# Rate at which VectorE's modulation steps are given out: 1.05 per projection tile instead of 0.7

## The chip, the cores and the metric

One core of a Trainium2 chip runs the whole kernel. The metric is the device time of one execution in microseconds (us), the median of several. Engines: TensorE (PE, with its weight loads as PEld), VectorE (DVE), ScalarE (ACT), GpSimd (POOL), and SyncE (SP), whose queue issues nearly all loads from HBM.

## The reference

Two layers, three groups of 128 tokens (one prompt group, two groups of latents, 384 tokens in all), width 1024, all in float32. What matters here:

```python
# mod = silu(c) @ ada_w[l] + ada_b[l], for two conditioning vectors: c_ctx (prompt), c (latents)
shift1, scale1, gate1, shift2, scale2, gate2 = jnp.split(mod[:, None, :], 6, axis=-1)
h = x * (1.0 + scale1) + shift1
mix, new_state = mixing_sublayer(h, p, init, latent)
x = layer_norm(DEEPNORM_ALPHA * x + gate1 * mix, p['ln1_w'], p['ln1_b'])
h = x * (1.0 + scale2) + shift2
a, gt = jnp.split(h @ p['ffn_w13'], 2, axis=-1)
ff = (jax.nn.silu(gt) * a) @ p['ffn_w2']
x = layer_norm(DEEPNORM_ALPHA * x + gate2 * ff, p['ln2_w'], p['ln2_b'])
```

`mod` of layer 1 depends on nothing but the conditioning vectors and the weights, so it can be computed at any time before layer 1 starts. It is a product of two vectors with a 1024 x 6144 matrix.

## The kernel before

**Products in two halves.** Every weight tile is split into a high and a low part in float32r: ScalarE casts the raw tile (`whi`, line 220), VectorE subtracts (`wlo`, line 221). TensorE then makes three matmuls where one would do (lines 270 to 272: high x high, low x high, high x low). A tile `wlo` is either 8 x 128 columns, made by two instructions of 128 x 512 from two raw tiles (`wcols`), or 2 x 512 columns, made by one instruction of 128 x 1024 (`wrows`). There are 3 buffers of raw tiles (`wraw`), 5 of `whi`, 4 of `wlo`.

**The FFN of a layer** runs in three parts of 8, 6 and 8 blocks of 128 hidden channels. Each part is `ffn_in` (columns of `ffn_w13` in chunks of 256: two tiles of the gate, then two tiles of the linear half, 24 matmuls of 384 columns each) and then `proj` (two halves of the output, three token groups each, 512 columns per matmul). For a gate tile ScalarE computes `sig`; for a linear tile VectorE multiplies (`gf`, line 1050), ScalarE casts (`fAh`) and VectorE subtracts (`fAl`, line 221). In `proj` VectorE multiplies the result by the gate vector (`gmix`, line 516) and adds it to `x` (lines 518 and 520).

**Layer 1's modulation on VectorE.** Two thirds of layer 1's `mod` (columns 0 to 4095, that is b = 0 and b = 1 of three) are not computed on TensorE but accumulated on VectorE while layer 0's FFN runs. The work is cut into 32 units. A unit loads 512 KB of `ada_w` (`wadv`, line 425, two buffers under the tag `wada`) and makes four instructions on VectorE: for each of 2 rows of 128 input channels and 2 conditioning vectors, accumulate weight x scalar into `adacc` (the first two of a group are line 477, all others line 479). Four units make one group of 512 columns. `close` then sums a group over partitions on TensorE (line 434, eight matmuls), the fourth group adds the bias (`mrows`, line 442), and `fin` transposes on TensorE (line 455) and copies to `modT` (line 456). The load of a unit is issued by the step of the unit before it:

```python
units = [(b, g, k) for b in bs for g in range(4) for k in range(0, KT, 2)]
...
                if k == 2 and i >= 4:
                    close(*units[i - 4][0:2])
            return go

        adq.extend(one(i) for i in range(len(units)))
        adq.extend([lambda: None, lambda: close(*units[-1][0:2]), lambda: None, lambda: None])
```

That is 36 steps in the queue `adq`, and two `fin` steps that are put into it on the way: 38. The third part (b = 2) is made on TensorE during layer 1 (`ada_steps`, lines 389 and 392).

**What sets the order.** The code emits instructions in program order; `tick` runs after every tile of a product and emits steps from `adq` by the rate `ADV`. The framework then places the instructions on the engines: an instruction whose operands are ready in its plan may be placed ahead of earlier ones, and the resulting order on each engine and on the SP queue is fixed. So the rate sets where a step is emitted, and the placement can move it some way from there.

```python
rate["aacc"] += w * rate["ada"]
while rate["aacc"] >= 1.0:
    rate["aacc"] -= 1.0
    if adq:
        adq.pop(0)()
```

The rate is set after the first `ffn_in` of layer 0. From there the ticks are 6 (first `proj`), 12 (second `ffn_in`), 6 (second `proj`), 16 (third `ffn_in`): 40. Before the last `proj` of layer 0 whatever is left in the queue is emitted at once:

```python
while adq:
    adq.pop(0)()
```

Of the kernel before, what the change touches and what calls it, by code (L numbers as in the profile page):

```python
# [33 lines left out]
M6 = 11  # L34
WRAW = 3
WADA = 2
ADV = 0.7
TAPS1, TAPS2 = 2.6, 3.2
FILL = 0.3
LEADN = 4  # L40
# [60 lines left out]
def tile_kernel(ctx: ExitStack, tc: tile.TileContext, a: dict, o: list):  # L101
# [1096 lines left out]
    for l in range(DEPTH):  # L1198
# [20 lines left out]
        for k0, n in ((0, 8), (8, 6), (14, 8)):  # L1219
            fA = ffn_in(l, h2, k0, n, lead if k0 == 0 else None)  # L1220
            if l == 0:
                rate["ada"] = ADV
            if lc2 is None:
# [58 lines left out]
```

## Time and profile before

| | |
|---|---|
| median of 3 runs | 1459.12 us (1458.92 to 1459.28) |
| the profiled execution, its own time | 1461.46 us |
| its span, first to last instruction | 1458.9 us |
| PE busy in the span | 1414.8 us |
| DVE busy in the span | 1004.5 us |
| mean granted TensorE clock | 0.989 of full speed |

The profile is of one execution. A duration of a matmul there overlaps the next one; the distance from start to start is what a matmul costs in a stream. The granted clock is 1.00 at 2.4 GHz and 0.50 at 1.2 GHz. Layer 0's FFN ends, and the last `proj` of layer 0 begins, some 720 us into the span.

### The profile page before, as it was taken

How to read it: one execution, taken by the hardware profiler on the slowest of the kernel's cores; microseconds unless marked ns; L12 is line 12 of the kernel's file. 1: busy time of each engine (PE TensorE's matmuls, PEld its weight loads, DVE VectorE, ACT ScalarE, POOL GpSimd, SP SyncE). 2: the span in 40 equal slices, each digit the busy share in tenths (PEclk: the TensorE clock that was granted, in tenths of full speed). 3: DMA queues.
4: the chain of work that ended last, by engine and by line, in shares of the span. 5: the costliest groups of instructions: out<-in, count | busy, mean ns of one | idle time of the engine just before them, and what ended most of it. 6: DMA issues, size and time to landing. Idle time of an engine off the chain costs nothing.

```text
span 1458.9 us, 20684 instructions
## 1 busy us (share of the span) xinstructions
PE 1414.8 (97%) x7990; PEld 1296.2 (89%) x7990; DVE 1004.5 (69%) x1976; ACT 590.2 (40%) x1090; POOL 67.5 (5%) x106
## 2 busy tenths in 40 slices
PE   6999999999999999999799999899999999999997
PEld 4799999989998999989677999899999889898996
DVE  3455798987987656897674559879886666544447
ACT  2445458423535333333134465544335254242430
POOL 1000002000100000000100010110000000000000
PEclk8999999999999999999899999999999999999999
DMA  9575254465473444666655442342535526243441
GB/s 323 170 233 177 95 138 158 144 230 175 160 273 101 150 162 136 217 189 202 217 143 165 154 149 66 84 123 87 164 99 170 173 73 205 86 157 100 145 159 43
DMA packets 141745, 226.09 MB, mean 155 GB/s; under 512 B 13304, under 2 KB 63032, under 8 KB 141648
## 3 DMA queue, kind: packets, MB, share of 16 engines
q1 hardware_dynamic: 140048, 222.65, 47.6%
q0 software_dynamic: 1600, 2.14, 0.5%
q8 instruction: 62, 1.02, 0.3%
q14 instruction: 35, 0.29, 0.1%
HBM read 221.05 MB, written 3.71 MB: 154 GB/s over the span
## 4 chain that ended last, share of the span: by engine, by line
PE 82%; DVE 9%; DMA 5%; ACT 1%; issue 1%; POOL 1%; SPq 0%; DVEq 0%; POOLq 0%; ACTq 0%
PE ps L270 24%; PE ps L271 24%; PE ps L272 24%; DMA wraw<-in_in_w_dram 3%; DVE wlo L221 2%; PE adaps L392 1%; DMA wadv<-in_ada_w_dram 1%; DVE cacc L870 1%; PE vacc L270 1%; PE vacc L271 1%; PE vacc L272 1%; DMA wada<-in_ada_w_dram 1%; DMA adaq<-in_ada_w_dram 1%; DVE adacc L479 1%; PE adaps L1108 1%
## 5 line engine op out<-in xcount | busy, mean ns | idle before, releaser
L220 ACT CAST whi<-wraw 128x512 fp32r<-128x512 f32 (+1 forms) x484 | 337.5, 723 | 591.9 <-PE ps L271 223.0
L221 DVE TENSOR_TENSOR wlo<-wraw,whi 128x512 fp32r<-128x512 f32 (+1 forms) x484 | 383.3, 813 | 176.2 <-ACT whi L220 75.6
L270 PE MATMUL ps<-h1h,whi 128*128 128x384 f32 x896 | 305.9, 342 | 4.6 <-DVE rpa L820 2.8
L272 PE MATMUL ps<-h1h,wlo 128*128 128x384 f32 x896 | 300.3, 336 | 1.0 <-DVE wlo L221 0.9
L271 PE MATMUL ps<-h1l,whi 128*128 128x384 f32 x896 | 299.6, 335 | 0.0
L270 PE MATMUL ps<-h2h,whi 128*128 128x384 f32 x576 | 193.4, 336 | 0.0
L272 PE MATMUL ps<-h2h,wlo 128*128 128x384 f32 x576 | 192.5, 334 | 0.0
L271 PE MATMUL ps<-h2l,whi 128*128 128x384 f32 x576 | 192.4, 334 | 0.0
L270 PEld LDWEIGHTS ps<-h1h,whi 128*128 128x128 f32 x896 | 168.4, 188 | 20.1 <-issue 8.4
L272 PEld LDWEIGHTS ps<-h1h,wlo 128*128 128x128 f32 x896 | 168.4, 188 | 2.1 <-DVE wlo L221 2.0
L271 PEld LDWEIGHTS ps<-h1l,whi 128*128 128x128 f32 x896 | 168.5, 188 | 0.1
L870 DVE SCALAR_TENSOR_TENSOR cacc<-u,cwt,cacc 128x399 f32<-128x399 f32 x232 | 144.7, 629 | 1.8
L270 PEld LDWEIGHTS ps<-h2h,whi 128*128 128x128 f32 x576 | 108.1, 188 | 1.1 <-issue 1.0
L271 PEld LDWEIGHTS ps<-h2l,whi 128*128 128x128 f32 x576 | 108.1, 188 | 0.2
L272 PEld LDWEIGHTS ps<-h2h,wlo 128*128 128x128 f32 x576 | 108.1, 188 | 0.0
L270 PE MATMUL ps<-whi,fAh 128*128 128x512 f32 x264 | 104.2, 395 | 0.0
L271 PE MATMUL ps<-wlo,fAh 128*128 128x512 f32 x264 | 103.8, 393 | 0.0
L272 PE MATMUL ps<-whi,fAl 128*128 128x512 f32 x264 | 103.7, 393 | 0.0
L516 DVE TENSOR_TENSOR gmix<-ps,lnc 128x512 f32<-128x512 f32 x48 | 33.1, 689 | 79.9 <-PE ps L272 79.9
L479 DVE SCALAR_TENSOR_TENSOR adacc<-wadv,cs,adacc 128x512 f32<-128x512 f32 x112 | 78.7, 746 | 4.4 <-DMA wadv<-in_ada_w_dram 4.4
L270 PEld LDWEIGHTS ps<-whi,fAh 128*128 128x128 f32 x264 | 50.3, 190 | 12.1 <-issue 1.9
L272 PEld LDWEIGHTS ps<-whi,fAl 128*128 128x128 f32 x264 | 50.1, 190 | 10.6
(318 smaller groups left out, 2019.4 us busy)
## 6 DMA issues: line engine op xcount, KB each, us to landing
wraw<-in_in_w_dram SPq DMA_DIRECT2D x64, 1024.0 KB
wraw<-in_ffn_w_dram SPq DMA_DIRECT2D x76, 512.0 KB
wraw<-in_ffn_w_dram SPq DMA_DIRECT2D x28, 1024.0 KB
wada<-in_ada_w_dram SPq DMA_DIRECT2D x48, 512.0 KB
wadv<-in_ada_w_dram SPq DMA_DIRECT2D x32, 512.0 KB
wraw<-in_out_w_dram SPq DMA_DIRECT2D x8, 1024.0 KB
adaq<-in_ada_w_dram SPq DMA_DIRECT2D x8, 512.0 KB
wraw<-in_mlstm_out_w_dram SPq DMA_DIRECT2D x4, 1024.0 KB
```

The lines of the kernel that those rows point to most:

```text
L220: nc.scalar.copy(hi, src)
L221: tt(lo, src, hi.bitcast(F32), op=ALU.subtract)
L270: mm(out, sh, vh, start=(first and i == 0), stop=False)
L271: mm(out, sh, vl, start=False, stop=False)
L272: mm(out, sl, vh, start=False, stop=(last and i == n - 1))
L392: mm(st["ps"][32 * g:32 * g + 32, :], cs[:, k, :], wts[g], start=(k == 0), stop=(k == KT - 1))
L479: stt(ac[:, m, :], wt[:, kk, :], c_, ac[:, m, :], op0=ALU.mult, op1=ALU.add)
L516: tt(g, ps, lc[0 if t == 0 else 1, hf], op=ALU.mult)
L870: tc.keep_in_program_order(stt(ac, u[:, k:k + CW], wk, ac, op0=ALU.mult, op1=ALU.add))
L1108: mm(ps[32 * g:32 * g + 32, s * 256:(s + 1) * 256], cs[:, k, :], tiles[u // 6][:, u % 6, :], start=(k < 4), stop=(k >= 4))
```

## The change

```diff
-ADV = 0.7
+ADV = 1.05
```

With 40 ticks, 0.7 gives out 28 of the 38 steps and 1.05 gives out all of them, the last at the 37th tick (37 x 1.05 = 38.85). No instruction is added or taken away: each engine has the same number before and after. Their order is the same up to the last tile of the first `proj` and again from the last `proj` on.

**Place 1, the end of the third `ffn_in` and the start of the last `proj`, on TensorE.** `ps_6655` is the last tile of `ffn_in`, `ps_6787` the first of `proj`. Before:

```order
L272 MATMUL ps_6655<-h2h_4209,wlo_6607 128x384
L434 MATMUL adaps_6397<-adacc_6591,one2_84 32x128 x8
L434 MATMUL adaps_6397<-adacc_6698,one2_84 32x128 x8
L455 MATMUL ps_6748<-cc_75,mrows_6735 128x128 x4
L270 MATMUL ps_6787<-whi_6769,fAh_6005 128x512
L271 MATMUL ps_6787<-wlo_6770,fAh_6005 128x512
```

Now (the last tile of `ffn_in` is called `ps_6725`):

```order
L270 MATMUL ps_6725<-h2h_4209,whi_6690 128x384
L271 MATMUL ps_6725<-h2l_4210,whi_6690 128x384
L272 MATMUL ps_6725<-h2h_4209,wlo_6691 128x384
L270 MATMUL ps_6787<-whi_6769,fAh_6083 128x512
L271 MATMUL ps_6787<-wlo_6770,fAh_6083 128x512
```

The last two closes and the transposes of the second `fin` no longer stand between the two products. The eight closes now stand spread from the end of the first `proj` to the middle of the third `ffn_in`.

The same place on VectorE; `gf_6637` and `gf_6680` belong to the last two tiles of `ffn_in`, `wlo_6784` is the last weight tile of the first half of `proj`. Before:

```order
L1050 TENSOR_TENSOR gf_6637<-ps_6612,sig_6560 128x384
L221 TENSOR_TENSOR wlo_6780<-wraw_6777,whi_6779 128x1024
L221 TENSOR_TENSOR fAl_6008<-gf_6637,fAh_6007 128x384
L477 TENSOR_SCALAR adacc_6698<-wadv_6690,cs_80 128x512 x2
L479 SCALAR_TENSOR_TENSOR adacc_6698<-wadv_6690,cs_80,adacc_6698 128x512 x2
L479 SCALAR_TENSOR_TENSOR adacc_6698<-wadv_6696,cs_80,adacc_6698 128x512
L1050 TENSOR_TENSOR gf_6680<-ps_6655,sig_6587 128x384
L479 SCALAR_TENSOR_TENSOR adacc_6698<-wadv_6696,cs_80,adacc_6698 128x512
L221 TENSOR_TENSOR fAl_6008<-gf_6680,fAh_6007 128x384
L479 SCALAR_TENSOR_TENSOR adacc_6698<-wadv_6696,cs_80,adacc_6698 128x512 x2
L479 SCALAR_TENSOR_TENSOR adacc_6698<-wadv_6703,cs_80,adacc_6698 128x512 x4
L221 TENSOR_TENSOR wlo_6784<-wraw_6777,whi_6783 128x1024
```

Now:

```order
L1050 TENSOR_TENSOR gf_6721<-ps_6696,sig_6645 128x384
L221 TENSOR_TENSOR wlo_6780<-wraw_6777,whi_6779 128x1024
L221 TENSOR_TENSOR fAl_6086<-gf_6721,fAh_6085 128x384
L1050 TENSOR_TENSOR gf_6750<-ps_6725,sig_6678 128x384
L221 TENSOR_TENSOR wlo_6784<-wraw_6777,whi_6783 128x1024
L221 TENSOR_TENSOR fAl_6086<-gf_6750,fAh_6085 128x384
```

No accumulate step is left here; the last one now stands ahead of the third of the eight linear tiles of the third `ffn_in`.

**Place 2, the second `ffn_in`, on VectorE.** From the product of a chunk's first linear tile on. Before:

```order
L1050 TENSOR_TENSOR gf_5427<-ps_5402,sig_5350 128x384
L221 TENSOR_TENSOR wlo_5562<-wraw_5557,whi_5561 128x512
L221 TENSOR_TENSOR wlo_5562<-wraw_5559,whi_5561 128x512
L221 TENSOR_TENSOR fAl_5306<-gf_5427,fAh_5305 128x384
L477 TENSOR_SCALAR adacc_5604<-wadv_5551,cs_80 128x512 x2
L479 SCALAR_TENSOR_TENSOR adacc_5604<-wadv_5551,cs_80,adacc_5604 128x512 x2
L479 SCALAR_TENSOR_TENSOR adacc_5604<-wadv_5602,cs_80,adacc_5604 128x512
L1050 TENSOR_TENSOR gf_5471<-ps_5446,sig_5377 128x384
L221 TENSOR_TENSOR wlo_5568<-wraw_5557,whi_5567 128x512
L221 TENSOR_TENSOR wlo_5568<-wraw_5559,whi_5567 128x512
L221 TENSOR_TENSOR fAl_5306<-gf_5471,fAh_5305 128x384
```

Now (`gf_5454` is the same tile as `gf_5427` was):

```order
L1050 TENSOR_TENSOR gf_5454<-ps_5429,sig_5372 128x384
L479 SCALAR_TENSOR_TENSOR adacc_5460<-wadv_5551,cs_80,adacc_5460 128x512 x2
L221 TENSOR_TENSOR fAl_5328<-gf_5454,fAh_5327 128x384
L479 SCALAR_TENSOR_TENSOR adacc_5460<-wadv_5551,cs_80,adacc_5460 128x512
L221 TENSOR_TENSOR wlo_5595<-wraw_5590,whi_5594 128x512
L221 TENSOR_TENSOR wlo_5595<-wraw_5592,whi_5594 128x512
L1050 TENSOR_TENSOR gf_5490<-ps_5465,sig_5405 128x384
L221 TENSOR_TENSOR wlo_5601<-wraw_5590,whi_5600 128x512
L221 TENSOR_TENSOR wlo_5601<-wraw_5592,whi_5600 128x512
L221 TENSOR_TENSOR fAl_5328<-gf_5490,fAh_5327 128x384
L477 TENSOR_SCALAR adacc_5637<-wadv_5584,cs_80 128x512 x2
L479 SCALAR_TENSOR_TENSOR adacc_5637<-wadv_5584,cs_80,adacc_5637 128x512 x2
```

At the first of these rows 13 of a group's 16 accumulate steps already lie behind it, where before the first of the group came after it: from the end of the first `proj` to the first projection tile of the second `proj`, VectorE now has 48 accumulate steps. Over the longer stretch up to the third linear tile of the third `ffn_in` it has 96 where it had 64.

**Place 3, the same time on the SP queue.** `wraw` are weight tiles, `wadv` the units' loads. Before:

```order
L258 DMA wraw_5638<-in_ffn_w13_dram 128x4x256
L425 DMA wadv_5681<-in_ada_w_dram 128x2x512
L258 DMA wraw_5640<-in_ffn_w13_dram 128x4x256
L258 DMA wraw_5728<-in_ffn_w13_dram 128x4x256
L425 DMA wadv_5722<-in_ada_w_dram 128x2x512
```

Now:

```order
L258 DMA wraw_5590<-in_ffn_w13_dram 128x4x256
L425 DMA wadv_5494<-in_ada_w_dram 128x2x512
L425 DMA wadv_5551<-in_ada_w_dram 128x2x512
L258 DMA wraw_5592<-in_ffn_w13_dram 128x4x256
L258 DMA wraw_5685<-in_ffn_w13_dram 128x4x256
L425 DMA wadv_5584<-in_ada_w_dram 128x2x512
L425 DMA wadv_5635<-in_ada_w_dram 128x2x512
L258 DMA wraw_5687<-in_ffn_w13_dram 128x4x256
```

Two units' loads (once three) now stand between two weight loads ten times until the units end.

## Rows read from the trace of the kernel before

**Rows 1.** The page: busy time, share of the span, instructions.

```profile
PE 1414.8 (97%) x7990; PEld 1296.2 (89%) x7990; DVE 1004.5 (69%) x1976; ACT 590.2 (40%) x1090; POOL 67.5 (5%) x106
```

**Rows 2.** PE's waits: releaser; us in total, times, longest.

```profile
PE adaps L434 <- DVE adacc L479: 9.8, 1, 9.8
```

**Rows 3.** Timeline around the end of layer 0's FFN: start us, us.

```profile
701.72 0.44 PE L270 MATMUL ps<-h2h,whi 128*128 128x384 f32 x1
...
706.08 0.64 PE L434 MATMUL adaps<-adacc,one 128*32 128x128 f32 x16
...
708.02 4.16 DVE L479 SCALAR_TENSOR_TENSOR adacc<-wadv,cs,adacc 128x512 f32<-128x512 f32 x6
...
712.10 1.22 DVE L221 TENSOR_TENSOR wlo<-wraw,whi 128x1024 fp32r<-128x1024 f32 x1
...
714.39 2.74 DVE L479 SCALAR_TENSOR_TENSOR adacc<-wadv,cs,adacc 128x512 f32<-128x512 f32 x4 [1.07 <-DMA wadv<-in_ada_w_dram]
...
716.52 1.32 PE L434 MATMUL adaps<-adacc,one 128*32 128x128 f32 x16 [9.79 <-DVE adacc L479]
...
718.72 1.11 PE L455 MATMUL ps<-cc,mrows 128*128 128x128 f32 x4 [0.89 <-DVE mrows L442]
...
719.49 0.78 PE L270 MATMUL ps<-whi,fAh 128*128 128x512 f32 x1
...
724.74 0.39 PE L270 MATMUL ps<-whi,fAh 128*128 128x512 f32 x1
```

**Rows 4.** Busy time by stretch there: PE, PEld, DVE, ACT, POOL, PEclk, DMA share.

```profile
720.00:722.00 2.00, 2.00 (x6) 1.55 (x5) 0.07 (x1) 0.00 (x0) 2.00 (x5) 0.50 0.73 241
726.00:728.00 2.00, 2.00 (x11) 1.64 (x10) 0.31 (x1) 0.00 (x0) 0.21 (x1) 1.00 0.01 4
```

**Rows 5.** The chain that ended last, 700 to 730 us: start, us.

```profile
709.46 4.83 DMA wadv<-in_ada_w_dram
...
724.10 0.43 PE ps L271
...
728.10 0.23 PE ps L272
```

**Rows 6.** PE's timeline around an earlier close and the earlier transposes.

```profile
597.81 0.34 PE L272 MATMUL ps<-h2h,wlo 128*128 128x384 f32 x1
...
598.66 0.44 PE L270 MATMUL ps<-h2h,whi 128*128 128x384 f32 x1
...
666.54 0.60 PE L455 MATMUL ps<-cc,mrows 128*128 128x128 f32 x4
666.90 0.42 PE L270 MATMUL ps<-h2h,whi 128*128 128x384 f32 x1
```

**Rows 7.** Busy time by stretch, all engines: PE, PEld, DVE, ACT, POOL, PEclk, DMA.

```profile
560.70:613.90 53.20, 53.20 (x328) 51.83 (x327) 42.01 (x68) 21.08 (x35) 0.00 (x0) 1.00 0.66 216
560.70:667.10 106.40, 106.40 (x629) 100.22 (x628) 88.56 (x140) 37.56 (x64) 0.00 (x0) 1.00 0.62 198
```

**Rows 8.** The same, first stretch, of line 479 and then of line 477 alone.

```profile
560.70:613.90 53.20, 18.01 (x27) 1.00 0.66 216
```

```profile
560.70:613.90 53.20, 1.75 (x4) 1.00 0.66 216
```

**Rows 9.** Timeline: first `proj`'s last gmix; second `proj`'s first matmul.

```profile
560.76 0.68 DVE L516 TENSOR_TENSOR gmix<-ps,lnc 128x512 f32<-128x512 f32 x1
```

```profile
611.25 0.39 PE L270 MATMUL ps<-whi,fAh 128*128 128x512 f32 x1
```

**Rows 10.** Waits of DVE and of the SP queue, 560 to 706 us.

```profile
DVE wlo L221 <- ACT whi L220: 13.3, 7, 3.9
```

```profile
SPq L425 <- DVE adacc L479: 71.3, 21, 6.8
```

**Rows 11.** A short PE wait in layer 1, and the clock behind it.

```profile
945.48 0.44 PE L270 MATMUL ps<-h1h,whi 128*128 128x384 f32 x1 [2.77 <-DVE rpa L820]
```

```profile
945.00:950.00 5.00, 4.52 (x23) 4.52 (x24) 4.24 (x12) 2.44 (x7) 1.22 (x3) 0.66 0.18 56
```

## The prediction

> **What bounds the kernel now.** I read the busy shares first. TensorE is busy for 97% of the span, VectorE for 69% [rows 1]. So only two things can shorten this kernel: less work on TensorE, or an end to one of its waits. The list of TensorE's waits, sorted by length, comes next, and its first row is one single wait of 9.8 us, for an accumulate step on VectorE [rows 2]. No other wait is near the change.
>
> The timeline shows where it lies. At 706.08 TensorE closes the seventh group, behind the last tile of layer 0's third ffn_in. Then it has the eighth close next in its queue, and that needs VectorE's last steps, which run at 708.02 and 714.39 [rows 3]. The close begins at 716.52, the transposes of the second fin at 718.72, and the first matmul of the last proj at 719.49 [rows 3]. The reader is to see that proj doesn't need any of this: its operands are weights and the FFN's activations. It only stands behind the close in TensorE's queue.
>
> The clock has fallen in the meantime. In 720 to 722 us the granted clock is 0.50 (1.2 GHz), in 726 to 728 it is 1.00 (2.4 GHz) [rows 4]. The chain shows the price: a matmul of 512 columns takes 0.43 us up to 724.5 and 0.23 us afterwards [rows 5].
>
> **The change part by part.**
>
> *The gap goes.* The seventh close ends at 706.08 + 0.64 = 706.72 and proj begins at 719.49 [rows 3]: 12.8 us. Without steps, closes and transposes at this place, proj follows the last tile directly. What is late next? The last tile's product, cast and subtraction on VectorE and ScalarE are needed only for the eighth of proj's eight steps of three matmuls, 7 x 3 x 0.23 = 4.8 us in. The wlo that before came at 712.10, behind six steps [rows 3], now stands right behind gf. It is needed 6 x 3 x 0.23 = 4.1 us in and takes 1.2. Neither makes TensorE wait. Term: **-12.8**.
>
> *The clock stays up.* From 719.49 to 724.74 twelve matmuls ran at 0.43 us (5.25 / 0.43 = 12.2) [rows 3, 5]. At 0.23 they take 2.7. Term: **-2.5**.
>
> *What moves back onto TensorE's path.* One close and one fin are now among the tiles. Around an earlier close two neighbouring matmuls start at 597.81 and 598.66, where 0.17 is usual, and the one behind it comes 0.1 late: 0.8 us. Earlier transposes cost 666.90 - 666.54 = 0.36, and 0.1 behind them [rows 6]. Term: **+1.3**. So the gain is 14.0 us if VectorE carries its steps elsewhere without making TensorE wait.
>
> *Can it?* This is the disputed cost. Two budgets decide.
>
> First budget, up to the second proj. From the gmix at 560.76 to the first matmul of the second proj at 611.25 [rows 9] TensorE didn't wait at all (53.20 busy of 53.20), and VectorE was busy for 42.0 of 53.2 us [rows 7]. In that time it made 27 steps of line 479 in 18.01 us, 0.667 each, and 4 of line 477 in 1.75, 0.44 each [rows 8]. By the order shown, 42 and 6 now come before the FFN's last low half (fAl) of this stretch is done: 15 x 0.667 + 2 x 0.44 = 10.9 more. The bias addition mrows comes in (0.7, like other operations of 512 elements), and one wlo of 1.2 goes out behind it [rows 3]. The sum is 42.0 + 10.9 + 0.7 - 1.2 = 52.4, and without waits VectorE is done at 560.7 + 52.4 = 613.1. TensorE wants this fAl in its sixth step of proj. The start at 611.25 moves by two more closes, 1.6, and five steps and two matmuls are 17 x 0.23 = 3.9: 616.7. **3.6 us to spare.**
>
> Second budget, up to the third linear tile of the third ffn_in. VectorE was busy for 88.56 of 106.4 us [rows 7]. 32 steps more are 28 x 0.667 + 4 x 0.44 = 20.4, in sum 109.0, so without waits it ends at 669.7. The last weight tile that it makes in this time is the first of the next chunk. TensorE ended the third linear tile at 666.54 [rows 6]; three closes more are 2.4, the fin that now comes earlier is 0.4, the fourth linear tile takes 4.3 (701.72 to the close at 706.08 [rows 3]), and the low half is the next tile's third matmul, 0.3: 673.9. **4.2 us to spare.** VectorE will be busy nearly all the time.
>
> *What eats the budgets: waits of VectorE itself.* A unit's load is issued when the unit two before it has been used up, since there are two buffers. A load took 4.83 us to land [rows 5]. Where only four steps and two half wlo (0.6 each) lie between, 4 x 0.667 + 1.2 = 3.9 us, VectorE waits for 0.9 to 1.1. By the order this happens at two places within the first budget, and once more, behind a load of 1 MB, in the second (0.8). So 2.1 and 2.9 us of waits, less than 3.6 and 4.2. The bounds of this unknown: nothing at best, and at worst the 13.3 us that VectorE waited for whi (weights that landed late) between 560 and 706 [rows 10], on top of these. I take the lower value. Those waits came where no step was there to fill them; now four to eight steps (2.7 to 5.3 us) mostly stand between the wlo that frees a raw buffer and the one that needs the next load. For a load that takes a little longer I put in 0.5 us.
>
> **The sum.** -12.8 - 2.5 + 1.3 + 0.5 = -13.5 us, against a span of 1458.9. The profiled execution's own time was 1461.46, 2.3 above the median of the runs, which is all outside what changes here; so 1459.1 - 13.5 = **1445.6 us**.
>
> A rule of the Trainium skill speaks against it (Perfetto Trace Analysis, Identifying the Most-Contended Engine): improve the engine with the highest occupancy first. By it this change, which touches only when a 69% engine works, would give nothing, 1459. The same page (Optimization Strategy) asks for the gaps of the saturated engine and what ends them, and the wait of 9.8 us is such a gap; here I follow the second rule.
>
> **The rivals.**
>
> *VectorE becomes the bound in the stretch (forecast partly eaten).* For it: 109.0 us of work in 106.4 + 2.4 us. With waits W in all, TensorE loses W - 4.2. At a W of 9.4, midway between 5.5 and 13.3, that is 5.2. A single longer wait can cost the clock too: behind a wait of 2.77 us in layer 1 the granted clock was 0.66 over 5 us, which is 1.7 us of lost work [rows 11]. So 14.0 - 5.2 - 1.7 = 7.1 gained: 1452.0. By the skill's page "TensorE: Matmul & The Clock Gate" (HAM oscillation) that price is paid anew at each idle stretch that is long enough; several of them would each add another 1.7.
>
> *Slower than before: the SP queue.* One mechanism: on SP two units' loads stand ahead of a weight load, ten times. A unit's load waits there for VectorE to free its buffer (71.3 us over 21 waits, longest 6.8 [rows 10]), and the weights behind it wait too, so that wlo, and in the end TensorE, waits for weights. VectorE's mean wait for late weights was 13.3 / 7 = 1.9 us [rows 10]. If it comes at all ten places, W is 19 + 2.9 = 21.9, TensorE loses 17.7, and the kernel takes 3.7 more: 1462.8. It decides from (14.0 + 4.2 - 2.9) / 10 = 1.5 us per place on. Against it: the steps that fill these times, as above, and TensorE's 53.20 of 53.20 with the same queue before.
>
> *No change: something else holds proj at 706.* The weights of its first half or the activations could be late too. Against it: their wlo is a single instruction of 1.2 us, held up by the steps in front of it, and nothing else on the list of waits stands there. The skill's first rule above would come to the same time.
>
> **Chances.** Forecast (14.0 gained, at most some 4 lost again), 1444.5 to 1449.5: 0.70. VectorE as the bound, 1449.5 to 1456: 0.20. No change, within 0.2% (2.9 us, about what a measurement of this kernel can tell from nothing): 0.05. Slower: 0.04. Faster than the forecast's range: 0.01. The range holds the forecast and most of the first rival: 1444.3 to 1452.5. Faster 0.91, same 0.05, slower 0.04.
>
> **What the profile will show.** Right, if TensorE's wait for line 479 is gone, if the last proj begins within 1 us of the last ffn_in tile and near 706, if the granted clock stays 1.00 there, and if VectorE is over 95% busy from 561 to 667 with TensorE's idle time in it below 1 us. Wrong in the disputed part, if TensorE waits for wlo or fAl (line 221) in that stretch, first at the start of the second proj (some 613 to 617), or for whi behind late weights. The forecast fails if those waits add up to more than 5 us.

## The result, and the profile after

The changed kernel took 1448.46 us in the median of six runs (1445.98 to 1450.80), the kernel before 1459.20 in six runs beside it (1458.83 to 1461.83). The ratio is 0.9921, with a 95% interval from 0.9909 to 0.9932. In a second comparison it was 0.9906 (0.9892 to 0.9919). So it is faster, by 10 to 16 us as the two intervals have it (medians 10.7 and 13.3 us apart); 13.5 were forecast. The profiled execution took 1446.28 us, its span 1444.2.

The page's row of busy times. VectorE does the same work in a shorter span. Of the 14.7 us by which the two spans differ, 3.0 are busy time of TensorE and 11.7 its idle time:

```profile
PE 1411.8 (98%) x7990; PEld 1295.3 (90%) x7990; DVE 1003.2 (69%) x1976; ACT 590.8 (41%) x1090; POOL 67.5 (5%) x106
```

TensorE's waits, the longest ones, after the change (releaser; us in total, times, longest). The wait of 9.8 us for line 479 that led the argument [rows 2] is not in the list any more. Between 553 and 730 us the list of this execution is empty:

```profile
PE ps L1092 <- DMA x<-in_x_prompt_dram: 7.1, 1, 7.1
PE vacc L270 <- DVE h1l L1127: 3.2, 1, 3.2
PE rvo L824 <- DVE rpa L819: 2.1, 2, 1.7
```

TensorE's timeline at the seam where the gap was. The last matmul of the third ffn_in starts at 707.91, the first of the last proj 0.18 us behind it, where [rows 3] had 706.72 (the seventh close's end) and 719.49:

```profile
707.91 0.33 PE L272 MATMUL ps<-h2h,wlo 128*128 128x384 f32 x1
708.09 0.39 PE L270 MATMUL ps<-whi,fAh 128*128 128x512 f32 x1
```

Busy time by stretch (PE, PEld, DVE, ACT, POOL, granted clock, DMA share, GB/s). The first two rows answer to [rows 7]: VectorE's 42.0 and 88.6 us have become 51.35 and 103.53, which is 97% of either stretch, and TensorE is still busy for all of it. The last two answer to [rows 4]: the granted clock is 1.00 (2.4 GHz) where it was 0.50.

```profile
560.70:613.90 53.20, 53.20 (x341) 51.68 (x341) 51.35 (x84) 20.58 (x35) 0.00 (x0) 1.00 0.79 257
560.70:667.10 106.40, 106.40 (x651) 99.28 (x651) 103.53 (x167) 35.50 (x60) 0.53 (x1) 1.00 0.73 231
...
710.00:720.00 10.00, 10.00 (x49) 7.42 (x47) 3.29 (x6) 0.00 (x0) 0.00 (x0) 1.00 0.40 105
720.00:730.00 10.00, 10.00 (x48) 8.20 (x45) 8.21 (x9) 4.22 (x4) 0.00 (x0) 1.00 0.72 181
```

VectorE's own waits and SP's, 560 to 706 us, as in [rows 10]. VectorE's wait for late weights fell from 13.3 to 4.1 us, and SP's wait for a unit's buffer from 71.3 to 54.1. Some other waits of SP rose, most of all that of line 226 until VectorE frees a raw tile (12.2 to 25.2 us), but TensorE's empty list above shows that it waited for none of these weights. The rival that weights come late behind the units' loads would have shown longer waits for late weights:

```profile
DVE wlo L221 <- ACT whi L220: 4.1, 2, 2.7
DVE adacc L479 <- DMA wadv<-in_ada_w_dram: 1.9, 3, 0.9
```

```profile
SPq L425 <- DVE adacc L479: 54.1, 22, 4.3
```

The two budgets, read off the timeline. The first: VectorE makes the disputed low half at 614.41 to 614.97, and TensorE's sixth step of the second proj uses it at 616.74. So 1.8 us were to spare; 3.6 less 2.1 of waits, 1.5, were forecast:

```profile
614.41 0.56 DVE L221 TENSOR_TENSOR fAl<-gf,fAh 128x384 fp32r<-128x384 f32 x1
```

```profile
616.74 0.39 PE L272 MATMUL ps<-whi,fAl 128*128 128x512 f32 x1
```

The second: the first weight tile of the next chunk is made by the first two of three halves in one row, and so is done at about 669.7. TensorE uses it in its third matmul behind the fourth linear tile, at 673.92. So 4.2 us were to spare; 4.2 less 2.9 of waits, 1.3, were forecast:

```profile
668.44 1.89 DVE L221 TENSOR_TENSOR wlo<-wraw,whi 128x512 fp32r<-128x512 f32 x3
```

```profile
673.92 0.33 PE L272 MATMUL ps<-h2h,wlo 128*128 128x384 f32 x1
```

**What was open.** The two profiles differ by 15.2 us in their own times, the medians by 10.7, and the changed kernel's runs spread over 4.8 us. Two theories go into the experiments. **T1** is the prediction's: the whole gain is the wait at the close and the half clock behind it, the filled stretch costs TensorE nothing, and the spread lies elsewhere. **T2** is the rival "VectorE becomes the bound" in a weaker form: the filled VectorE makes TensorE wait in some executions, and that eats a part of the gain.

### The profile page after: what moved, and what is told of

It reads as the page before. It is cut to its first block, busy times and chain, and to the rows that moved or that the text cites. A ratio compares the mean times of both kernels' runs of the same rounds, so it can differ in the third digit from the quotient of the medians.

```text
span 1444.2 us, 20672 instructions
## 1 busy us (share of the span) xinstructions
PE 1411.8 (98%) x7990; PEld 1295.3 (90%) x7990; DVE 1003.2 (69%) x1976; ACT 590.8 (41%) x1090; POOL 67.5 (5%) x106
## 4 chain that ended last, share of the span: by engine, by line
PE 83%; DVE 8%; DMA 6%; issue 1%; ACT 1%; POOL 1%; SPq 0%; DVEq 0%; POOLq 0%; ACTq 0%
PE ps L270 25%; PE ps L272 25%; PE ps L271 25%; DMA wraw<-in_in_w_dram 3%; DVE wlo L221 2%; DMA adaq<-in_ada_w_dram 1%; PE adaps L392 1%; DVE cacc L870 1%; DMA wada<-in_ada_w_dram 1%; PE vacc L270 1%; PE vacc L272 1%; PE vacc L271 1%; DMA wadv<-in_ada_w_dram 1%; PE adaps L1108 0%; PE ps L905 0%
## 5 line engine op out<-in xcount | busy, mean ns | idle before, releaser
L270 PEld LDWEIGHTS ps<-whi,fAh 128*128 128x128 f32 x264 | 49.6, 188 | 12.2 <-issue 2.1
```

The source lines that it names most:

```text
L270: mm(out, sh, vh, start=(first and i == 0), stop=False)
```

## The experiments

The edits of experiments 2, 4 and 5 are shown against the kernel before, the others against the changed kernel. T1 and T2 are the two theories just named, S1 and S2 the two guesses on the spread that stand in the expectation of the first further profile of the kernel before.

**1. The changed kernel and the kernel before again, for more profiles.** No edit. First the changed kernel:

> The changed kernel once more, unchanged, against the kernel before. Its first six runs went from 1446.0 to 1450.8 us, and the one that was profiled was among the shortest. T1 (all of the gain is the wait at the close ahead of the last proj and the half clock behind it; TensorE doesn't wait for VectorE in the stretch from 561 to 667): 1448, from 1446 to 1451, and a profile of a longer run shows its extra 2 to 4 us outside of that stretch, in waits for loads or in the other layer, as in runs of the kernel before. T2 (VectorE is filled to 97% in the stretch, and in some executions a load that lands a little later makes TensorE wait there): the same median, but a profile of a longer run shows 2 us or more of waits for lines 221 or 479 between 553 and 710.

Measured: 1446.87 us (1445.85 to 1448.83), ratio 0.9906 (0.9892 to 0.9919); its profiled run, at 1445.85, was a short one. A third profile of it and three more of the kernel before were taken to find the spread:

> The changed kernel, unchanged, for a third profile. T1 with S1: layer 0 ends at 743.9 within 0.5, with no wait of TensorE for lines 221 or 479 between 553 and 730, whatever its time is; what it takes more than 1446 lies in layer 1's retention. T2 (the filled VectorE makes TensorE wait in some executions): if this is a longer run, layer 0 ends 1 us or more later than 743.9.

> The kernel before, unchanged, for a second profile. Between its first profile and the changed kernel's, 13.9 us lie up to the end of layer 0, but the medians of the runs differ by 11 to 13, and both kernels' runs spread over 4 to 5 us. T1 with the spread in layer 1 (S1): up to the end of layer 0 every execution of the kernel before is as the first, with a wait of about 9.8 for line 479 and twelve products at half clock, the last product of layer 0 at 757.8 within 0.5; and the runs differ in layer 1's retention, where the same instructions took 45.5 to 50.2 us from the first product of line 824 to the first of the last chunk in the profiles so far. S2: the clock falls behind the wait only in some executions; then some profile of the kernel before ends layer 0 some 4 us earlier (753.7).

> The kernel before once more, for a third profile: as before_b. S1: layer 0 ends at 757.8 within 0.5; S2: in some of these profiles at about 753.7, with no product at half clock.

> The kernel before once more, for a fourth profile: as before_b. S1: layer 0 ends at 757.8 within 0.5; S2: in some of these profiles at about 753.7, with no product at half clock.

Single times: the changed kernel 1446.89, the kernel before 1461.62, 1460.95 and 1459.72. In each profile I read two matmuls: the last one of the first proj, up to where the order of instructions is the same in both kernels, and the last one of layer 0, from where it is the same again. The kernel before, first, second and fourth profile (the third had 559.52 and 758.01):

```profile
559.51 0.39 PE L272 MATMUL ps<-whi,fAl 128*128 128x512 f32 x1
...
757.79 0.39 PE L272 MATMUL ps<-whi,fAl 128*128 128x512 f32 x1
```

```profile
560.99 0.39 PE L272 MATMUL ps<-whi,fAl 128*128 128x512 f32 x1
...
759.06 0.39 PE L272 MATMUL ps<-whi,fAl 128*128 128x512 f32 x1
```

```profile
558.07 0.39 PE L272 MATMUL ps<-whi,fAl 128*128 128x512 f32 x1
...
755.87 0.39 PE L272 MATMUL ps<-whi,fAl 128*128 128x512 f32 x1
```

The changed kernel, first profile (the second had 559.65 and 743.93, the third 559.64 and 743.92):

```profile
559.60 0.39 PE L272 MATMUL ps<-whi,fAl 128*128 128x512 f32 x1
...
743.88 0.39 PE L272 MATMUL ps<-whi,fAl 128*128 128x512 f32 x1
```

The stage between took 198.3, 198.1, 198.5 and 197.8 us before, and 184.3 us in all three profiles after. So **the change is worth 13.5 to 14.2 us in the stage that it touches**, in every profile. Of 40 runs of the kernel before the mean is 1460.4 (1457.3 to 1462.8), of 11 of the changed kernel 1447.8 (1445.9 to 1450.8): 12.7 us. T2 finds no support: the three profiles of the changed kernel end layer 0 within 0.05 us of each other, and the list of TensorE's waits between 553 and 730 us is empty in all three. But none of them is of a run above 1446.9, so what the longest runs do there wasn't seen.

Both guesses on the spread were too simple. S1 asked for an end of layer 0 within 0.5 us of 757.8 in the kernel before; it varied by 3.2, and 2.9 of that is there already at the end of the first proj. S2 is wrong too: the clock fell in all four profiles. Only how long it stayed down differs: the last proj took 38.3, 38.1, 37.5 and 37.3 us from its first to its last matmul, against 35.8 in the changed kernel, so 1.5 to 2.5 us. The Trainium skill (TensorE: Matmul & The Clock Gate, Part 1: The HAM clock gate) says of a kernel's start that the number of slow matmuls changes from run to run; these four profiles show it behind a wait in the middle.

The spread that S1 placed in layer 1's retention is there. From the first product of line 824 to the fourth, over the same instructions in the same order, the kernel before took 46.6 to 47.1 us, the changed kernel's three profiles 46.6, 45.5 and 47.5, the experiments below that have the same order there 45.9 to 51.0. The changed kernel's first two profiles, first and fourth product:

```profile
913.49 0.38 PE L824 MATMUL rvo<-rv,rpa 128*128 128x128 f32 x2
...
960.08 0.38 PE L824 MATMUL rvo<-rv,rpa 128*128 128x128 f32 x2
```

```profile
913.53 0.38 PE L824 MATMUL rvo<-rv,rpa 128*128 128x128 f32 x2
...
959.05 0.38 PE L824 MATMUL rvo<-rv,rpa 128*128 128x128 f32 x2
```

**2. TensorE kept at work during the wait.** At 0.7; takes the clock out of the gain. Nobody reads the products added here.

```diff
+                ps = psum()
+                hi0 = h2.part(0)[0]
+                for i in range(52):
+                    mm(ps[:, 0:T], hi0[:, 0:P], hi0, start=(i == 0), stop=(i == 51))
                 while adq:
                     adq.pop(0)()
```

> The kernel before (0.7), with 52 products of 128x384 that nobody reads put on TensorE ahead of the drain's closes, so that it works (52 x 0.173 = 9.0 us) where it waited 9.8 us for the accumulate steps. Nothing else changes: the last proj begins at the same time, 719.5. It parts my term of 12.8 (the wait and what stands in it) from that of 2.5 (twelve products at half clock behind it). T1: the wait for line 479 is below 1 us, the granted clock stays 1.00 after 719.5, and the time is 2.5 less than before: 1457 (1456 to 1458), that is 0.9983 of it. Rival (the 12 slow products are not an effect of the idle time, or the clock costs nothing): 1459 to 1460, no change.

Measured: 1458.55 us (1456.59 to 1462.53, 11 runs); ratio 0.9989 (0.9980 to 0.9998). Its timeline of TensorE: the added products, the two closes, the transposes, the first matmul of the last proj and the last of layer 0. Then VectorE's last four steps, and the busy times of a stretch:

```profile
706.02 9.18 PE L1234 MATMUL ps<-h2h 128*128 128x384 f32 x52
715.12 1.41 PE L434 MATMUL adaps<-adacc,one 128*32 128x128 f32 x32
717.42 0.65 PE L455 MATMUL ps<-cc,mrows 128*128 128x128 f32 x4 [0.88 <-DVE mrows L442]
717.83 0.48 PE L270 MATMUL ps<-whi,fAh 128*128 128x512 f32 x1
...
753.69 0.39 PE L272 MATMUL ps<-whi,fAl 128*128 128x512 f32 x1
```

```profile
713.32 2.74 DVE L479 SCALAR_TENSOR_TENSOR adacc<-wadv,cs,adacc 128x512 f32<-128x512 f32 x4
```

```profile
712.00:718.00 6.00, 4.99 (x56) 4.21 (x55) 4.68 (x7) 0.00 (x0) 0.46 (x2) 1.00 0.69 222
```

The clock stays at 1.00, and layer 0 ends at 753.69, 4.1 us before the first profile of the kernel before. Of these, 2.4 lie in the last proj, as in my term: 35.9 us from its first to its last matmul instead of 38.3. The other 1.7 lie ahead of it, since proj begins at 717.83 and not, as expected, at 719.5, and only a part of them is the clock's. VectorE's last four steps begin at 713.32 here; in [rows 3] they waited 1.07 us for a unit's load and began at 714.39. From their start to proj it takes 4.5 us instead of 5.1, with the end of the close and the transposes at full clock. So of my 12.8 us for the gap 0.6 belong to the clock and 1.1 to that load. VectorE waited for it in all four profiles of the kernel before (0.7 to 1.1 us) and not here; whether the added products have to do with that stays open. The page TensorE: Matmul & The Clock Gate of the Trainium skill (HAM oscillation) says that a wait which brings the clock down is paid for again in slow products behind it; here that price was 3.0 us. The time lies between T1's 1456 to 1458 and the rival's 1459 to 1460: over whole runs only 1.6 us are left by the ratio (0.3 to 2.9). In the profiled run layer 1's retention took 50.2 us from the first to the fourth product of line 824 instead of 46.6. TensorE's waits there, 910 to 980 us, are for the same lines as in the other profiles, and a little longer. The granted clock in this stretch differs between profiles (0.93 here, 0.90 to 1.00 in all), but it doesn't order the times: 1.00 went with 46.6 us, 0.93 with 46.6 to 50.2. What lengthens the waits I couldn't find:

```profile
PE ps L270 <- ACT whi L220: 3.1, 1, 3.1
PE ps L270 <- DVE rpa L820: 3.0, 1, 3.0
PE rvo L828 <- DVE rpb L821: 1.7, 1, 1.7
```

**3. A little less than 1.05.** Lowers VectorE's density in the stretch.

```diff
-ADV = 1.05
+ADV = 0.95
```

> 0.95 steps a projection tile: still none of the eight closes is left to the drain, but VectorE's steps of the second projection's modulation are spread over some 10% more tiles, so that its share in the stretch is lower (about 93% instead of 97%). T1: the wait ahead of the last proj is gone just as in the changed kernel, so the same time within 1 us of it (1446 to 1450). T2: what TensorE loses now and then to the filled VectorE comes back, 1.5 to 3 us less than the changed kernel (1445 to 1446.5), with a smaller spread of the runs. A third way: the last steps end so late that the eighth close itself waits for its steps, then 1450 to 1456.

Measured: 1448.00 us (1445.54 to 1448.60), ratio 0.9909 (0.9895 to 0.9922), the same as the changed kernel, and with no smaller spread that four runs could show. VectorE was busy for 100.55 of the 106.40 us, 94.5% (93% expected). T1 holds, T2's 1445 to 1446.5 doesn't: no gain from a lower density shows.

**4. The rest given out among the last proj's tiles.** At 0.7, so that the stretch stays as it was.

```diff
-                while adq:
-                    adq.pop(0)()
-                fillers += ada_steps(1, 2)
-                rate["fill"] = FILL
+                rate["ada"] = 2.1
...
                 lead2 = proj(fA, w2, lc2, False, True, after2)
+                while adq:
+                    adq.pop(0)()
+                fillers += ada_steps(1, 2)
+                rate["fill"] = FILL
```

> 0.7 steps a tile as before, but what is left over is not taken in one piece ahead of the last proj: it is given out at 2.1 a tile among that proj's tiles. So the two closes move behind the wait's place, and the stretch from 561 to 667 stays as in the kernel before (VectorE 83%). T1: the gap of 12.8 us goes away and the half clock with it, less 1.3 for close and fin among tiles, and up to 2 where the steps hold up a weight tile of that proj: 1446 to 1450, as the changed kernel. T2 (filled stretch costs 2 to 3 us in the median): 1445 to 1446. If the place were not what counts, but the number of steps made earlier, it would stay near 1459.

Measured: 1447.11 us (1446.81 to 1449.65), ratio 0.9910 (0.9896 to 0.9923). The same gain on another way, without a filled stretch. In its timeline proj begins at 705.25 and the seventh close stands in it:

```profile
705.25 0.39 PE L270 MATMUL ps<-whi,fAh 128*128 128x512 f32 x1
...
716.26 0.65 PE L434 MATMUL adaps<-adacc,one 128*32 128x128 f32 x16
```

It ends layer 0 at 741.65, 2.2 us before the changed kernel. Of these, 0.8 are there already at the end of the first proj (558.77 instead of 559.60); for the rest, the third modulation's products, two groups of which (1.0 us each) stand in that proj there, begin only behind it here. Between 900 and 1000 us TensorE then waits for a weight tile, longer than for any one thing there in the changed kernel, and the advance is lost again:

```profile
PE ps L272 <- DVE wlo L221: 4.6, 1, 4.6
```

**5. The close moved behind proj on TensorE, VectorE's steps left ahead of it.** At 0.7; the eighth close and the sum move behind proj, and with them the start of the third modulation.

```diff
-                while adq:
+                while len(adq) > 4:
                     adq.pop(0)()
-                fillers += ada_steps(1, 2)
-                rate["fill"] = FILL
+                rate["ada"] = 0.0
...
                 lead2 = proj(fA, w2, lc2, False, True, after2)
+                while adq:
+                    adq.pop(0)()
+                fillers += ada_steps(1, 2)
+                rate["fill"] = FILL
```

> 0.7 steps a tile as before and the steps left over still ahead of the last proj on VectorE, but for the last four; the close of TensorE that waited for them, and the last sum, stand behind that proj's first tiles instead of ahead of it. So only the order on TensorE changes: VectorE still makes six steps ahead of proj's weight tile. T1: the wait in the close goes; TensorE waits instead for the weight tile behind six steps of 0.67 (4 us, of which the last linear tile covers part), 1 to 4 us, and the clock may hold: 1449 to 1453. A rival, that the gap is VectorE's backlog wherever the close stands: the same 9.8 us return as a wait for the weight tile, 1457 to 1460.

Measured: 1452.07 us (1450.35 to 1453.46), ratio 0.9939 (0.9925 to 0.9952). The time is T1's, but for a partly wrong reason. VectorE's timeline: six steps still run ahead of the last weight tile of proj's first half, which is done at 713.66:

```profile
708.28 4.24 DVE L479 SCALAR_TENSOR_TENSOR adacc<-wadv,cs,adacc 128x512 f32<-128x512 f32 x6
712.44 1.22 DVE L221 TENSOR_TENSOR wlo<-wraw,whi 128x1024 fp32r<-128x1024 f32 x1
```

Yet proj begins at 706.91, and TensorE doesn't wait at all until 742, where I expected 1 to 4 us for this tile: its queue has 19 products of the first tile of proj, then 10 of the second, and only then the five that need the late weights. So VectorE's backlog held up nothing here; what held up TensorE was that the close stood ahead of proj in its queue. One reservation belongs to it: proj's order isn't the one of the two main kernels, whose timelines show a tile's 24 products in line. The framework's placement put ten products of the second tile ahead of the five. In line, the first of them would have come at about 711.3, 2.4 us before its weights were done (an estimate: 706.91 + 19 x 0.23). So the order hides a backlog of about the size that I expected. TensorE's only wait between 700 and 745 us is now that of the transposes behind proj:

```profile
PE ps L455 <- DVE mrows L442: 1.5, 1, 1.5
```

The 4 to 5 us that are missing against the changed kernel show up behind layer 0: the retention begins at 916.22 instead of 913.49, and between 900 and 1000 us there is a wait of 6.2 us for a weight tile. Experiment 4, which also starts the third modulation later, had it too; that the later start is its cause wasn't tested.

**6. More steps a tile.** Tests the budgets from the other side: nothing left over, but earlier.

```diff
-ADV = 1.05
+ADV = 1.5
```

> 1.5 steps a projection tile instead of 1.05: nothing is left over for the drain, but the steps come earlier. By the order, 96 accumulate steps now stand ahead of the last linear tile of the second projection stage's FFN input, where the changed kernel has 80: 16 x 0.667 = 10.7 us more for VectorE up to the second proj. T1 with its budget (VectorE's slack up to there is what separates its last low half, done at 615.0 in the changed kernel's profile, from its use at 616.7, so 1.7 us): TensorE loses 10.7 - 1.7 = 9.0 there and nothing later, 1457 (1453 to 1460), with the wait on lines 221 near the start of the second proj or among the tiles ahead of it. Rival (VectorE's share isn't what counts, any rate without a rest is as good): 1447 to 1449, as 1.05.

```diff
-ADV = 1.05
+ADV = 2.5
```

> 2.5 steps a tile: all 128 accumulate steps stand ahead of the fifth row of linear tiles of the second FFN input, 48 more than in the changed kernel by its end (32 us of VectorE), 44 of them ahead of its first tiles. T1 with its budget: TensorE loses up to 32 - 1.7 = 30 us, less what VectorE has free during the first proj; 1468 to 1480, and TensorE's waits are for weights' low halves (line 221) from the first proj on. The half clock behind several such waits may add 1.7 each. Rival (any rate without a rest): 1447 to 1450.

Measured: 1459.06 us (1456.89 to 1463.76), ratio 0.9993 (0.9983 to 1.0002), and 1479.11 us (1478.17 to 1480.97), ratio 1.0128 (1.0115 to 1.0142). At 1.5 the gain is gone, at 2.5 the kernel is 1.3% slower than before. TensorE's waits at 1.5, 600 to 700 us, and two stretches of it:

```profile
PE ps L271 <- DVE wlo L221: 3.8, 2, 3.4
PE adaps L434 <- DVE adacc L479: 2.7, 4, 1.1
PE ps L270 <- ACT whi L220: 1.1, 1, 1.1
```

```profile
620.00:640.00 20.00, 15.39 (x89) 10.78 (x81) 18.95 (x31) 3.03 (x5) 0.00 (x0) 0.96 0.59 174
640.00:660.00 20.00, 18.75 (x93) 15.70 (x94) 19.97 (x31) 2.39 (x4) 3.38 (x8) 0.86 0.67 198
```

VectorE is the bound here, as the rival had it, and the last proj begins at 722.00 instead of 708.09: 13.9 us lost in the stage where the budget gave 9.0. Of these, 2.0 are there already at the end of the first proj (561.56 instead of 559.60), and the profiled run was the longest of ten; by the medians and means of the runs some 11 us are lost. What the budget left out stands in these rows: the closes themselves wait for accumulate steps (2.7 us), and the granted clock falls to 0.96 and 0.86 over 20 us each. At 2.5 the waits for weights between 553 and 680 us come to 18.9 us, one of them 11.4, and the clock falls to 0.66:

```profile
PE ps L272 <- DVE wlo L221: 18.9, 5, 11.4
```

```profile
620.00:640.00 20.00, 11.20 (x65) 9.97 (x66) 15.48 (x31) 2.49 (x6) 4.28 (x9) 0.66 0.71 209
```

Against the changed kernel 31 us are lost (30 expected).

**7. More work on VectorE at 1.05.** Tests how much the stretch still has to spare.

```diff
+                if k % 4 == 0:
+                    stt(ac[:, 1, :], ac[:, 1, :], 0.0, ac[:, 1, :], op0=ALU.mult, op1=ALU.add)
                 if k == 2 and i >= 4:
                     close(*units[i - 4][0:2])
```

> The changed kernel, and in every second of the 32 accumulate units one more operation of 128x512 on VectorE (times 0, plus itself, so that nothing changes in the sums): 16 x 0.667 = 10.7 us more for VectorE, all of it in the filled stretch or just ahead of it, and nothing else. T1 with its budgets: some 5 of them (3.4 us) come ahead of the second proj, where 1.7 us are to spare, and 14 (9.3 us) ahead of the third linear tile of the third FFN input, where VectorE was done at 669.6 or so and TensorE needs it at 673.9, 4.3 to spare: TensorE loses 5.0 in all, 1453 (1450 to 1456). Rival (VectorE still has room, since 69% of it is busy over the span): 1447 to 1449. Other rival (VectorE has no room at all, T2): 10 us lost, 1457 to 1459.

Measured: 1453.07 us (1452.05 to 1455.45), ratio 0.9946 (0.9931 to 0.9961). Its last proj begins 4.7 us later than in the changed kernel (5.0 expected):

```profile
712.82 0.39 PE L270 MATMUL ps<-whi,fAh 128*128 128x512 f32 x1
```

TensorE's waits of this kernel, 553 to 730 us:

```profile
PE ps L272 <- DVE wlo L221: 1.7, 2, 1.4
PE adaps L434 <- DVE adacc L479: 0.4, 2, 0.2
```

The 4.7 us can't be set against 10.7, since the added operations didn't all come where the expectation put them. VectorE's timeline has four of the 16 at 380 to 428 us, far ahead of the stretch, as it has the first 32 of the 128 accumulate steps there; 12 of them, 12 x 0.667 = 8.0 us, lie between 565 and 676 us. The order isn't the same either: the placement moved eight of the ordinary steps (5.3 us) behind the third linear tile of the third ffn_in, where the changed kernel has none, and TensorE's products stand in another order too. And 0.25 of the 4.7 us are there already at the end of the first proj (559.85 instead of 559.60). So of 8.0 us more for VectorE in this stage about 3.5 fit in and 4.5 cost TensorE time; neither rival (nothing lost, all lost) holds. That the loss came out near the forecast is luck in part: 14 added operations were counted up to the third linear tile, and 11 came there. Up to the second proj nothing is lost beyond the 0.25 us (613.00 against 612.75, 1.7 expected), and all the rest behind it. The waits listed make up some half of the 4.7; the rest shows as no single gap.

## Why the prediction was right

**The gap** was forecast at -12.8 and +1.3. The last proj begins 11.4 us earlier than in the first profile of before, where 11.5 was the sum. Experiments 4 and 5 show the reason: with the close out of TensorE's way, proj begins within 1 us of the last ffn_in tile, whether VectorE's steps come earlier, later or at the same place.

**The clock** was forecast at -2.5 behind the gap: 2.5 in the first profile and 1.5 to 2.5 in the four. Experiment 2 adds that another 0.6 us of the gap were the clock's as well, and 1.1 a wait of VectorE for a unit's load; the two terms were right in sum.

**The filled stretch** was the disputed cost, and I put in 0.5 for it. It costs nothing that a profile shows. The first budget was close: VectorE 97% busy (above 95% forecast), waits for units' loads of 1.9 us (2.9 forecast), the low half 1.8 us ahead of its use (1.5 forecast). The second was too narrow: 4.2 us to spare instead of 1.3. Experiment 7, where about 3.5 us more fit in, goes with that. Experiment 6 shows what lies beyond it. The rival "VectorE becomes the bound" was the right mechanism for a larger rate; at 1.05 its point isn't reached. Its price in the prediction rests on waits of 9.4 us, midway between 5.5 and 13.3; no row gives the 5.5, and the worst case named before it was 13.3 on top of 2.9.

**The SP queue** was the rival on the other side. Its sign, waits for whi behind late weights, went down instead of up.

**The size over whole runs** is the weakest point. The stage gained 13.5 to 14.2 us, the runs 12.7 by the means, and the median of the first six 10.7. The sum took the stage's gain for the kernel's. Experiments 2, 4 and 5 show that layer 1 can give back some 2 to 5 us; in experiment 2, where the same instructions run in the same order, it was for no reason that I could find. Whether it takes 1 us from the changed kernel's longer runs, or whether the difference between 13.9 and 12.7 is chance with a spread of 5 us, stays open.

I also read the 2.3 us between the profiled execution and the median as something outside the change. That holds: the stage took 198.3 us in it and 197.8 to 198.5 in the four profiles, and that execution was one of the longer runs (1457.3 to 1462.8 for the same kernel).

The prediction set a rule against the change: improve the engine with the highest occupancy first (the Trainium skill, Perfetto Trace Analysis, Identifying the Most-Contended Engine), which was to mean that nothing is gained. That was a misreading. The engine with the highest occupancy is TensorE, and ending its wait of 9.8 us is an improvement of that engine, so the measured gain doesn't speak against the rule. The same page's Optimization Strategy also advises to interleave stretches in which different engines are the limit. Here VectorE worked off six steps in the 4.16 us from 708.02 on while TensorE waited [rows 3], and the change moved that work under TensorE's. The rows agree up to 97% of VectorE; 1.5 steps a tile show the end of it.

## What to carry to other kernels

When an engine that is busy for 98% waits once, look at what stands ahead of the useful instruction in its own queue: here the next product needed none of what the close waited for, and moving the work for it gave all of the gain, moving only the close and the sum behind it two thirds. Before you fill another engine's idle time, make its budget up to each point where the bound engine uses its results, its own waits included, and then expect the gain to end abruptly: 1.05 gave all of it, 1.5 nothing, 2.5 a loss. And compare a stage's gain in several profiles with that of whole runs, since a later stage can swallow a part.

## What the runs showed of the hardware that was not expected

- VectorE was 96 to 97% busy for 106 us (101.94 to 103.53 in three profiles) beside a TensorE that lost nothing (106.40 busy of 106.40 in each).
- After an idle time of 9.5 to 9.8 us the granted clock was 0.50 in all four profiles of the kernel before, but it cost between 1.5 and 2.5 us behind the gap, though the same matmuls followed.
- The same instructions in the same order took 45.5 to 51.0 us in layer 1's retention, at a granted clock of 0.90 to 1.00 and with waits of TensorE for VectorE and ScalarE of up to 3.4 us each that change places from one execution to the next, while the stage of the change took 184.3 us in three profiles out of three.
